# The memory's values made before the second mixer, and the router and the experts' tokens taken from x itself

## The chip, the cores and the metric

The kernel runs on one core of a Trainium2 chip. The metric is the device time of one execution in microseconds (us), taken as the median of several runs. The core has a matrix engine (TensorE, PE in the profile), a vector engine (DVE), a scalar engine (ACT), GpSimd (POOL), and SyncE (SP), which here issues nearly all the transfers from DRAM.

## What is computed

Two transformer blocks follow one another on 256 tokens of width 1024, all in float32. The first has two layers: an mLSTM mixer with a dense FFN, and then an HGRN2 mixer with eight experts, of which each token takes two. The second block is attention with three branches, one of which reads a memory of 256 rows, and a dense FFN. What the change touches is this part (`ada` is a linear map of a conditioning vector that gives six vectors for each layer):

```
hn = rmsnorm(x, norm1_w) * (1 + scale1) + shift1
x  = x + gate1 * hgrn2_mixer(hn)                 # ends with "@ h_w_out", the out-projection
hn = rmsnorm(x, norm2_w) * (1 + scale2) + shift2
logits = hn @ router_w                           # 1024 x 8
top_logits, top_idx = top_k(logits, 2);  top_w = softmax(top_logits)
x  = x + gate2 * sum_e gates[:, e] * swiglu(hn, wg[e], wu[e], wd[e])
...
mkv = rms_norm(mem, g_mem) @ w_mem_kv            # 1024 x 1024: keys 0..511, values 512..1023
mk, mv = split(mkv);  mk = rms_norm(heads(mk), g_k_mem)
```

## The kernel before

The activations are kept transposed, as `x` of 128 partitions by 8 chunks by 256 tokens. Every float32 operand of a large product is split into a high and a low part (`whi`/`wlo` for weights, `act_hi`/`act_lo` for activations); ACT writes the high part as a rounded copy and DVE the low part as a difference. `mm3` then issues three passes, high by high, low by high, high by low. Small products are issued by `mm` on plain float32 operands; each such instruction stands as two matmuls in the trace. In an order listing it is still one, so `x4` there is `x8` in the trace.

Weights come as tiles of up to 1 MB in the order that `all_weights` (line 186 on) yields them. `load` puts each in one of four `raw` buffers (some in one of two `raw2` buffers), `parts_of` splits it into one of three `whi` and three `wlo` buffers, and `prepare` keeps a depth of one or two tiles split ahead of the products. Between the FFN's products one tile of `ada_w` after another is also loaded, into `raw2`, and summed by DVE (`ada_step`).

A scheduler puts each engine's instructions in an order that it decides when the program is built; each engine then works through its list strictly in that order, and waits at an instruction until its inputs and its buffer are there. `hold` and `behind` keep a step back until a named instruction has been issued: after a normalization (`normed`) the next tiles' splits wait for its last instruction.

A normalization sums squares over all 1024 values of a token: ACT squares each chunk, POOL adds the first of them up, PE sums over partitions with a column of ones (`token_sums`), DVE works out the inverse root in about ten small steps (`rsqrt`, names `st1v`, `st1y`), PE spreads it over the partitions (`spread`: a broadcast column times the identity), and DVE and ACT write the normalized chunks.

Around the change the program runs thus. After the first FFN comes `normed` and then `hgrn`, the second mixer. In the out-projection that ends the mixer, `memory_norm` loads the memory `memT`, sums its squares and writes its split `yeh`/`yel`. Then `normed` writes the experts' input, `moe` makes the logits with the split router weights (24 products), turns the input from chunks to token order with 32 products with `identr`, takes the two largest logits of each token (`first_max`, a chain of small DVE steps), and counts tokens for each expert (five products on `mask`). `memory` issues 48 products for the keys K, `head_norm` normalizes these, and 48 more products make the values V. A branch (line 1159) then asks whether an expert has over 128 tokens; every engine passes it. Behind it `experts` gathers the tokens for each pair of experts with 32 products on `disp`.

Of the kernel before, what the change touches and what calls it, by code (L numbers as in the profile page):

```python
# [20 lines left out]
P = 128  # L21
# [117 lines left out]
class Kernel:  # L139
# [61 lines left out]
    def all_weights(self):  # L201
# [19 lines left out]
        yield from ffn(a["ffn_w_gate"], a["ffn_w_up"], a["ffn_w_down"], FF)  # L221
        yield from columns("h_w_in", 1024, 1536, 0, 512, 2048, 2560, 3072, 3584)
        yield from columns("h_w_out", 0, 512)
        yield from columns("w_mem_kv_2", 0, 512)
# [331 lines left out]
    def out_proj(self, act, gate, between=None):  # L556
        self.stat_begin()
        self.depth = 2
        for g in range(2):
            self.proj_t(act, between=between, ends=lambda banks, cb: self.resid(banks[cb // 2][:, cb % 2, :], 4 * g + cb, gate))  # L560
# [142 lines left out]
    def run(self):  # L703
# [4 lines left out]
        with tc.tile_pool(name="cond", bufs=1) as pool:  # L708
# [19 lines left out]
            self.ffn(act, self.mod_part(0, 5), lambda f: self.ada_step(f * 30 / 33))  # L728
            self.tap("x2", x)
            self.ada_owed = 0.0  # L730
            self.hold = [[self.last_resid]] * 2
            self.ada_until(32)
            with tc.tile_pool(name="hgrn", bufs=1) as hgrn:
                act = self.normed(x, self.stat_end(), self.gain(1, 1, self.vec("n1", 8, 8)), self.mod_part(1, 0))
                act = self.hgrn(hgrn, act)
            self.ada_until(48)
        self.wide = False
        with tc.tile_pool(name="moe", bufs=1) as pool:
            kv = self.ctx.enter_context(tc.tile_pool(name="memkv", bufs=1, side="right"))
            self.mk = self.t(kv, [P, 4, S], "mk")  # L740
            self.mv = self.t(kv, [P, 2, 512], "mv")
            mem = self.memory_norm(pool)
            self.out_proj(act, self.mod_part(1, 2))
            self.tap("x3", x)
            act = self.normed(x, self.stat_end(), self.gain(1, 4, self.vec("n2", 8, 8)), self.mod_part(1, 3))
            self.moe(pool, act, mem)
# [19 lines left out]
    def memory_norm(self, pool):  # L766

        m = self.raw(self.a["memT"].rearrange("p (c s) -> p c s", c=DC))
        self.stat_begin()
# [319 lines left out]
    def moe(self, pool, act, mem):  # L1089
        nc, a, tc = self.nc, self.a, self.tc  # L1090
        lgp = self.bank()
        lgt = self.t(pool, [8, S], "lgt")
        lg = self.t(pool, [P, 2, 8], "lg")
        self.small(lgp[:8, :S], self.router_w, act)
        nc.vector.tensor_copy(lgt, lgp[:8, :S])
        for tt in range(2):
            nc.tensor.transpose(lgp[:, S + tt * 8 : S + tt * 8 + 8], lgt[:, tt * P : (tt + 1) * P], self.cst("ident")[:8, :8])
        nc.vector.tensor_copy(lg.rearrange("p a b -> p (a b)"), lgp[:, S : S + 16])

        xt = [self.t(pool, [P, 2, D], n, 1, F32R) for n in ("xth", "xtl")]  # L1100
        for tt in range(2):
            for half in range(2):
                for i in range(2):
                    ps = self.bank()
                    for c in range(4):
                        self.mm(ps[:, c * P : (c + 1) * P], act[i][:, half * 4 + c, tt * P : (tt + 1) * P], self.identr, c == 0)
                    dst = xt[i][:, tt, half * 512 : (half + 1) * 512]
                    if i == 0:
                        self.act(dst, ps, AF.Copy)
                    else:  # L1110
                        nc.vector.tensor_copy(dst, ps)
# [17 lines left out]
        e2, w1, w2 = (sm(n, (P, 2)) for n in ("e2", "w1", "w2"))  # L1129
# [352 lines left out]
```

## Time and profile before

| | |
|---|---|
| runs, median (lowest to highest) | 1469.27 us (1464.16 to 1472.32), 3 runs |
| the profiled execution's own time | 1472.68 us |
| its span in the trace | 1470.9 us |
| mean granted clock of PE, share of full | 0.969 |
| PE busy | 1416.9 us, 96% of the span |
| DVE, ACT, POOL busy | 1122.9, 837.9, 33.8 us |
| transfers | 343.49 MB, mean 234 GB/s |

Busy time of PE counts matmuls that overlap in the pipeline, so the work of a product is read from the distance between the starts of two neighbours. The numbers of the stretch in which the change lies are in three parts of the span: the middle and the end of the first FFN (about 265 to 379 us), the second out-projection (524 to 548 us), and the routing up to the experts' first product (548 to 598 us).

### The profile page before, as it was taken

The numbers are of one execution on the slowest core, as the hardware profiler recorded it, in microseconds if no ns is written. First come the engines' busy times: TensorE is split into PE (matmuls) and PEld (weight loads), VectorE is DVE, ScalarE is ACT, GpSimd is POOL, SyncE is SP. The second block draws the span as 40 slices with busy tenths as digits, with TensorE's granted clock in tenths as the row PEclk, the third lists the DMA queues.
The fourth block names the chain that finished last, engine by engine and source line by source line (L and its number), as shares of the span: only waits on it lengthen the run. The fifth ranks groups of instructions, "written<-read, shape, count | busy, mean of one in ns | idle before, by whom it ended". The sixth has DMA issues, their size and how long they took to land.

```text
span 1470.9 us, 23270 instructions
## 1 busy us (share of the span) xinstructions
PE 1416.9 (96%) x9356; PEld 1293.3 (88%) x9356; DVE 1122.9 (76%) x1741; ACT 837.9 (57%) x1197; POOL 33.8 (2%) x38
## 2 busy tenths in 40 slices
PE   5999899999899998999999999999999999999998
PEld 4789899999899986888888888888878899999998
DVE  6875798888687867698798897888776777765554
ACT  2652454344695555777787777777555455544332
POOL 1000100000000020000000000000000000100000
PEclk7987899999899999899999999999999999999999
DMA  8975579998454144599799898996425344555542
GB/s 336 342 270 185 176 278 355 348 348 328 153 174 142 59 156 131 193 362 361 271 363 330 306 350 324 329 352 227 154 86 188 128 146 142 172 175 198 173 144 87
DMA packets 149507, 343.49 MB, mean 234 GB/s; under 512 B 5904, under 2 KB 27280, under 8 KB 149136
## 3 DMA queue, kind: packets, MB, share of 16 engines
q1 hardware_dynamic: 148240, 341.00, 65.9%
q8 instruction: 75, 1.23, 0.3%
q10 hardware_dynamic: 1152, 0.94, 0.2%
q14 instruction: 40, 0.33, 0.1%
HBM read 340.86 MB, written 1.05 MB: 232 GB/s over the span
## 4 chain that ended last, share of the span: by engine, by line
PE 57%; ACT 1%; DVE 1%; issue 0%; ACTq 0%
PE acc L165 38%; PE ps L165 17%; PE ps L1222 1%; ACT whi L175 0%; PE ps L1313 0%; DVE wlo L181 0%; PE ps L700 0%; ACT e L175 0%; ACT L175 0%; PE ps L1438 0%; DVE yel L178 0%; ACT yeh L175 0%; ACT sg L175 0%; DVE ss L679 0%; DVE nm L1306 0%
## 5 line engine op out<-in xcount | busy, mean ns | idle before, releaser
L181 DVE TENSOR_TENSOR wlo<-raw,whi 128x1024 fp32r<-128x1024 f32 (+2 forms) x564 | 647.2, 1184 | 147.7 <-ACT whi L175 147.0
L175 ACT ACTIVATE whi<-raw 128x1024 fp32r<-128x1024 f32 (+2 forms) x564 | 547.8, 1016 | 321.6 <-PE acc L165 183.5
L165 PE MATMUL acc<-act_hi,whi 128*128 128x256 f32 x1344 | 385.1, 288 | 2.7 <-ACT act_hi L175 2.4
L165 PE MATMUL acc<-act_lo,whi 128*128 128x256 f32 x1344 | 385.0, 287 | 0.0
L165 PE MATMUL acc<-act_hi,wlo 128*128 128x256 f32 x1344 | 383.1, 285 | 1.3 <-DVE wlo L181 1.3
L165 PEld LDWEIGHTS acc<-act_hi,whi 128*128 128x128 f32 x1344 | 258.6, 193 | 4.7 <-ACT act_hi L175 3.0
L165 PEld LDWEIGHTS acc<-act_hi,wlo 128*128 128x128 f32 x1344 | 258.9, 193 | 1.6 <-DVE wlo L181 1.5
L165 PEld LDWEIGHTS acc<-act_lo,whi 128*128 128x128 f32 x1344 | 259.0, 193 | 1.1 <-issue 0.4
L165 PE MATMUL acc<-whi,act_hi 128*128 128x512 f32 (+1 forms) x560 | 216.1, 386 | 1.8 <-DVE conv L178 1.7
L165 PE MATMUL acc<-wlo,act_hi 128*128 128x512 f32 (+1 forms) x560 | 215.2, 384 | 0.0
L165 PE MATMUL acc<-whi,act_lo 128*128 128x512 f32 (+1 forms) x560 | 214.5, 383 | 0.0
L165 PEld LDWEIGHTS acc<-whi,act_hi 128*128 128x128 f32 x560 | 105.2, 188 | 21.4 <-issue 2.2
L165 PEld LDWEIGHTS acc<-wlo,act_hi 128*128 128x128 f32 x560 | 105.2, 188 | 19.3 <-DVE wlo L181 0.6
L165 PEld LDWEIGHTS acc<-whi,act_lo 128*128 128x128 f32 x560 | 105.1, 188 | 18.8
L485 DVE SCALAR_TENSOR_TENSOR raw<-raw,cond 128x1024 f32<-128x1024 f32 x96 | 115.3, 1230 | 6.4 <-DMA raw<-in_ada_w_dram 6.4
L165 PE MATMUL ps<-hh,whi 128*128 128x256 f32 x352 | 99.6, 283 | 1.5 <-DVE x L178 1.5
L165 PE MATMUL ps<-hl,whi 128*128 128x256 f32 x352 | 99.5, 283 | 0.0
L165 PE MATMUL ps<-hh,wlo 128*128 128x256 f32 x352 | 99.4, 283 | 0.0
L165 PE MATMUL ps<-wlo,hth 128*128 128x512 f32 x176 | 69.0, 392 | 0.0
L165 PEld LDWEIGHTS ps<-hh,whi 128*128 128x128 f32 x352 | 67.4, 192 | 1.7 <-DVE x L178 1.7
L165 PE MATMUL ps<-whi,htl 128*128 128x512 f32 x176 | 68.8, 391 | 0.0
L165 PE MATMUL ps<-whi,hth 128*128 128x512 f32 x176 | 67.5, 393 | 0.0
(355 smaller groups left out, 1777.5 us busy)
## 6 DMA issues: line engine op xcount, KB each, us to landing
raw<-in_ada_w_dram SPq DMA_DIRECT2D x48, 1024.0 KB, 6.3
raw<-in_moe_w_down_dram SPq DMA_DIRECT2D x40, 1024.0 KB, 5.7
raw<-in_moe_w_up_dram SPq DMA_DIRECT2D x32, 1024.0 KB, 7.3
raw<-in_moe_w_gate_dram SPq DMA_DIRECT2D x32, 1024.0 KB, 7.6
raw<-in_w_in_dram SPq DMA_DIRECT2D x26, 1024.0 KB, 5.1
raw<-in_h_w_in_dram SPq DMA_DIRECT2D x16, 1024.0 KB, 5.7
raw<-in_m_w_in_dram SPq DMA_DIRECT2D x12, 1024.0 KB, 7.4
raw<-in_moe_w_gate_dram SPq DMA_DIRECT2D x16, 768.0 KB, 5.5
```

The costliest lines, as they stand in the source:

```text
L165: self.nc.tensor.matmul(out, l, r, start=start, stop=True, skip_group_check=True)
L175: return self.nc.scalar.activation(out, in_, f, **k)
L181: return self.nc.vector.tensor_tensor(out, a, b, op=op)
L485: last = self.nc.vector.scalar_tensor_tensor(w[:, i, :], in0=w[:, i, :], scalar=1.0, in1=self.cond, op0=ALU.mult, op1=ALU.mult, accum_out= ...
L1222: nc.tensor.transpose(hps[:, f * P : (f + 1) * P], h[:, f * P : (f + 1) * P], self.cst("ident"))
```

## The change

The values V are made right behind the first FFN. The memory is loaded and normalized in the middle of that FFN (at its 61st quarter step), the two tiles of `w_mem_kv` with V's columns come before the mixer's weights, and V goes to a DRAM tile, from which it is read back later. The memory is loaded and normalized a second time in the out-projection, for K. `memory_norm` now makes the scaled memory by a plain ACT copy, then a rounded ACT copy and a POOL subtraction, where it was one rounded ACT copy and one DVE step.

The experts' input is no longer normalized in chunks. `route_begin` multiplies the router weights by the gain (`gw`) and writes the gain as a diagonal matrix for each chunk (`gdiag`), both on POOL; spreads the shift over a row (`srow`, eight plain float32 products); and works out the shift's part of the logits (`sw`, eight more). `route_add` adds each chunk of x to the logits as soon as the out-projection has ended it, 16 plain float32 products in all. `moe` then turns x to token order with 16 plain float32 products on `gdiag`; the inverse root comes in per token, by DVE, as it reads the result.

In `experts` the 32 gathering products of a pair on `disp` now stand ahead of the small products of the gates (`gps`) and of the way back (`bps`), where they stood behind them.

```diff
@@ -219,9 +219,10 @@
...
+        yield from columns("w_mem_kv_2", 512)
         yield from columns("h_w_in", 1024, 1536, 0, 512, 2048, 2560, 3072, 3584)
         yield from columns("h_w_out", 0, 512)
-        yield from columns("w_mem_kv_2", 0, 512)
+        yield from columns("w_mem_kv_2", 0)
...
@@ -553,11 +554,23 @@
-    def out_proj(self, act, gate, between=None):
+    def out_proj(self, act, gate, between=None, also=None):
...
+            def products():
+                if also:
+                    also(c)
+                sums()
...
@@ -722,16 +735,30 @@
...
-            self.router_w = self.load_small(self.cp, "router_w")
+            self.router_w = self.load_small(self.cp, "router_w", True)[0]
...
+            self.mv_kept = dram.tile([P, 2, 512], F32, tag="mv", name="mv_kept", bufs=1)
+            with tc.tile_pool(name="mem", bufs=1) as pool:
+                mem = []
+
+                def between(f):
+                    self.ada_step(f * 30 / 33)
+                    mem.append(self.memory_norm(pool, "acc") if len(mem) == 60 else None)
+
+                self.ffn(act, self.mod_part(0, 5), between)
+                m, by = mem[60]
...
+                act = self.normed(x, self.stat_end(), self.gain(1, 1, self.vec("n1", 8, 8)), self.mod_part(1, 0))
+                mv = self.t(pool, [P, 2, 512], "mv")
+                for tt, bank in enumerate(self.proj_tok(m)):
+                    self.act(mv[:, tt, :], bank, AF.Copy, scale=by[:, tt, :])
+                nc.scalar.dma_start(self.mv_kept, mv)
             with tc.tile_pool(name="hgrn", bufs=1) as hgrn:
-                act = self.normed(x, self.stat_end(), self.gain(1, 1, self.vec("n1", 8, 8)), self.mod_part(1, 0))
                 act = self.hgrn(hgrn, act)
...
@@ -739,11 +766,12 @@
...
+            nc.scalar.dma_start(self.mv, self.mv_kept)
+            self.route_begin(pool)
             mem = self.memory_norm(pool)
-            self.out_proj(act, self.mod_part(1, 2))
+            self.out_proj(act, self.mod_part(1, 2), also=self.route_add)
             self.tap("x3", x)
-            act = self.normed(x, self.stat_end(), self.gain(1, 4, self.vec("n2", 8, 8)), self.mod_part(1, 3))
-            self.moe(pool, act, mem)
+            self.moe(pool, mem)
...
@@ -763,19 +791,23 @@
...
-        return self.scaled(m, self.vec("g_mem"), tiles), self.stat_tokens()
+        g = self.vec("g_mem")
+        for c in range(DC):
+            t = self.t(self.tp, [P, S], "sq", 4)
+            self.act(t, m[:, c, :], AF.Copy, scale=g[:, c : c + 1])
+            self.act(tiles[0][:, c, :], t, AF.Copy)
+            self.nc.gpsimd.tensor_tensor(tiles[1][:, c, :], t, tiles[0][:, c, :].bitcast(F32), op=ALU.subtract)
+        return tiles, self.stat_tokens()
...
     def memory(self, pool, act, by):
         self.head_norm(pool, self.proj_tok(act), 4, self.mk, self.vec("gk_mem"), by=by)
-        for tt, bank in enumerate(self.proj_tok(act)):
-            self.act(self.mv[:, tt, :], bank, AF.Copy, scale=by[:, tt, :])
...
@@ -1086,29 +1118,49 @@
...
+    def route_begin(self, pool):
...
+        nc.gpsimd.tensor_tensor(self.gw, self.router_w, g.unsqueeze(2).to_broadcast([P, DC, 8]), op=ALU.mult)
+        for c in range(DC):
+            nc.gpsimd.tensor_tensor(self.gdiag[:, c, :], self.cst("ident"), g[:, c : c + 1].to_broadcast([P, P]), op=ALU.mult)
+        for half in range(2):
+            ps = self.bank()
+            for i in range(4):
+                self.spread(ps[:, i * P : (i + 1) * P], shift[:, 4 * half + i : 4 * half + i + 1], i == 0)
+            self.act(self.srow[:, half * 512 : half * 512 + 512], ps, AF.Copy)
+        ps = self.bank()
+        self.lgp = ps[:, :16].rearrange("p (a e) -> p a e", a=2)
+        for c in range(DC):
+            self.mm(ps[:, 16:24], shift[:, c : c + 1].to_broadcast([P, P]), self.router_w[:, c, :], c == 0)
+        self.sw = self.t(self.cp, [P, 8], "sw")
+        self.act(self.sw, ps[:, 16:24], AF.Copy)
+
+    def route_add(self, c):
+        for tt in range(2):
+            self.mm(self.lgp[:, tt, :], self.x[:, c, tt * P : (tt + 1) * P], self.gw[:, c, :], False)
...
+                    self.mm(ps[:, c * P : (c + 1) * P], self.x[:, cc, tt * P : (tt + 1) * P], self.gdiag[:, cc, :], c == 0)
+                xps.append(ps)
+        r = self.stat_tokens()
         for tt in range(2):
...
+            self.stt(lg[:, tt, :], self.lgp[:, tt, :], r[:, tt, :], self.sw, ALU.mult, ALU.add)
...
-                for i in range(2):
-                    ps = self.bank()
-                    for c in range(4):
-                        self.mm(ps[:, c * P : (c + 1) * P], act[i][:, half * 4 + c, tt * P : (tt + 1) * P], self.identr, c == 0)
...
+        for n, ps in enumerate(xps):
+            half, tt = n // 2, n % 2
+            sl = slice(half * 512, half * 512 + 512)
+            t = self.t(self.tp, [P, 512], "h", 2)
+            self.stt(t, ps, r[:, tt, :], self.srow[:, sl], ALU.mult, ALU.add)
+            self.split(xt[0][:, tt, sl], xt[1][:, tt, sl], t)
...
+        self.wide = True
+        self.hold = [[routed]]
+        self.memory(pool, *mem)
         self.depth = 1
-        self.wide = True
-        self.memory(pool, *mem)
...
```

PE from the first FFN to the second mixer. Before: the FFN's last products (`ps`), the token sums, the spread, and the mixer's first products.

```order
L165 MATMUL ps_1943<-hh_3361,wlo_3370 128x256
L165 MATMUL acc_3479<-cst_base_69,sq_3524 128x1 x2
L165 MATMUL acc_3479<-cst_base_69,sq_3534 128x1 x2
L165 MATMUL acc_3479<-cst_base_69,sq_3545 128x1 x2
L165 MATMUL acc_3479<-cst_base_69,sq_3556 128x1 x2
L165 MATMUL acc_3479<-cst_base_69,sq_3567 128x1 x2
L165 MATMUL ps_3591<-cst_base_69,st1y_3579 128x128 x2
L165 MATMUL acc_3644<-act_hi_3596,whi_3425 128x256
```

After: the memory's normalized copy (`yeh`, `yel`) times V's weights stands between the sums.

```order
L165 MATMUL ps_1945<-hh_3441,wlo_3450 128x256
L165 MATMUL acc_3559<-cst_base_69,sq_3604 128x1 x2
L165 MATMUL acc_3708<-whi_3505,yeh_2443 128x512
L165 MATMUL acc_3559<-cst_base_69,sq_3614 128x1 x2
L165 MATMUL acc_3708<-wlo_3506,yeh_2443 128x512
L165 MATMUL acc_3708<-whi_3505,yel_2444 128x512
L165 MATMUL acc_3559<-cst_base_69,sq_3625 128x1 x2
L165 MATMUL acc_3709<-whi_3505,yeh_2443 128x512
L165 MATMUL acc_3709<-wlo_3506,yeh_2443 128x512
```

Further V products and the spread of the inverse root follow, eight products behind the last sum (a part):

```order
L165 MATMUL acc_3708<-wlo_3506,yeh_2443 128x512
L165 MATMUL acc_3708<-whi_3505,yel_2444 128x512
L165 MATMUL ps_3668<-cst_base_69,st1y_3656 128x128 x2
L165 MATMUL acc_3709<-whi_3505,yeh_2443 128x512
L165 MATMUL acc_3709<-wlo_3506,yeh_2443 128x512
```

The last V products and the mixer's first (`act_hi` is the normalized input):

```order
L165 MATMUL acc_3709<-wlo_3582,yeh_2443 128x512
L165 MATMUL acc_3709<-whi_3581,yel_2444 128x512
L165 MATMUL acc_3795<-act_hi_3673,whi_3712 128x256
L165 MATMUL acc_3795<-act_lo_3674,whi_3712 128x256
L165 MATMUL acc_3796<-act_hi_3673,whi_3712 128x256
```

The 48 V products stand between the FFN's last product and the mixer's first, 15 of them ahead of the spread and 33 behind it.

PE at the start of the second out-projection. `r4y` is the inverse root of the mixer's heads. Before, the rows on `sq` are the memory's sums:

```order
L165 MATMUL acc_5160<-act_lo_4459,whi_5034 128x256
L165 MATMUL ps_4821<-cst_base_69,r4y_4809 128x128 x4
L165 MATMUL ps_4827<-cst_base_69,r4y_4809 128x128 x4
L165 MATMUL ps_4969<-cst_base_69,sq_4984 128x1 x2
L165 MATMUL ps_4969<-cst_base_69,sq_4989 128x1 x2
L165 MATMUL ps_4969<-cst_base_69,sq_4993 128x1 x2
L165 MATMUL acc_5160<-act_hi_4458,wlo_5035 128x256
```

After, `mod` is the shift:

```order
L165 MATMUL acc_5235<-act_hi_4609,whi_4988 128x256
L165 MATMUL ps_4972<-cst_base_69,r4y_4960 128x128 x4
L165 MATMUL ps_4978<-cst_base_69,r4y_4960 128x128 x4
L165 MATMUL ps_5132<-cst_base_69,mod_77 128x128 x4
L165 MATMUL ps_5138<-cst_base_69,mod_77 128x128 x4
L165 MATMUL ps_5144<-router_w_1398,mod_77 128x8 x8
L165 MATMUL ps_5157<-cst_base_69,sq_5172 128x1 x2
L165 MATMUL ps_5157<-cst_base_69,sq_5177 128x1 x2
L165 MATMUL ps_5157<-cst_base_69,sq_5181 128x1 x2
L165 MATMUL acc_5235<-act_lo_4610,whi_4988 128x256
L165 MATMUL acc_5235<-act_hi_4609,wlo_4989 128x256
```

Eight spreads of the shift (two rows of four) and eight products of the shift with the router weights have come in between the spreads of `r4y` and the memory's sums.

PE at the branch. Before: V's last products, the branch, the gates' products, and then the gathering on `xth`/`xtl`.

```order
L165 MATMUL acc_5569<-wlo_5573,yeh_4997 128x512
L165 MATMUL acc_5569<-whi_5572,yel_4998 128x512
L1157 TENSOR_LOAD mosti_5469
L1159 COMPARE_AND_BRANCH
L165 MATMUL ps_5658<-gate_5454,disp_5657 128x1
L165 MATMUL ps_5670<-identr_75,disp_5657 128x128
L165 MATMUL ps_5658<-gate_5454,disp_5657 128x1
L165 MATMUL ps_5670<-identr_75,disp_5657 128x128
```

After: K's last products, the transposes of the normalized keys `h`, the branch, and the gathering.

```order
L165 MATMUL acc_5614<-whi_5463,yeh_5185 128x512
L165 MATMUL acc_5614<-wlo_5464,yeh_5185 128x512
L165 MATMUL acc_5614<-whi_5463,yel_5186 128x512
L713 MATMUL ps_5703<-cst_base_69,h_5701 128x128 x4
L713 MATMUL ps_5711<-cst_base_69,h_5709 128x128 x4
L1218 TENSOR_LOAD mosti_5583
L1220 COMPARE_AND_BRANCH
L165 MATMUL ps_5745<-disp_5738,xth_5550 128x256 x2
L165 MATMUL ps_5745<-disp_5738,xtl_5551 128x256 x2
```

V's 48 products are gone from here, and with them the work among which the transposes of the keys stood before: these now stand alone between K's last product and the branch.

## Rows read from the trace of the kernel before

**Rows 1.** The page: busy times, the chain that ended last, and the costliest DVE group

```profile
PE 1416.9 (96%) x9356; PEld 1293.3 (88%) x9356; DVE 1122.9 (76%) x1741; ACT 837.9 (57%) x1197; POOL 33.8 (2%) x38
...
PE 57%; ACT 1%; DVE 1%; issue 0%; ACTq 0%
...
L181 DVE TENSOR_TENSOR wlo<-raw,whi 128x1024 fp32r<-128x1024 f32 (+2 forms) x564 | 647.2, 1184 | 147.7 <-ACT whi L175 147.0
```

**Rows 2.** ACT in the first FFN, in time: start, duration, work, [idle before <-releaser]

```profile
266.54 2.01 ACT L175 ACTIVATE whi<-raw 128x1024 fp32r<-128x1024 f32 x2 [2.74 <-PE ps L165]
...
272.30 2.01 ACT L175 ACTIVATE whi<-raw 128x1024 fp32r<-128x1024 f32 x2 [3.75 <-PE ps L165]
```

**Rows 3.** Busy time by stretch in the FFN (length; PE, PEld, DVE, ACT, POOL; clock; DMA)

```profile
265.00:275.00 10.00, 10.00 (x87) 10.00 (x86) 6.97 (x10) 4.02 (x4) 0.00 (x0) 1.00 1.03 402
```

**Rows 4.** POOL in time: runs of five additions of squares

```profile
8.58 6.63 POOL L410 TENSOR_TENSOR sq<-sq,sq 128x256 f32<-128x256 f32 x5 [7.25 <-ACT sq L175]
...
520.99 4.02 POOL L410 TENSOR_TENSOR sq<-sq,sq 128x256 f32<-128x256 f32 x5 [148.28 <-ACT sq L175]
```

**Rows 5.** PE in time, from the FFN to the second mixer

```profile
370.37 0.28 PE L165 MATMUL ps<-hh,wlo 128*128 128x256 f32 x1
...
370.99 3.46 PE L165 MATMUL acc<-cst_base,sq 128*128 128x1 f32 x20 [0.34 <-POOL sq L410]
...
376.48 1.22 PE L165 MATMUL ps<-cst_base,st1y 128*128 128x128 f32 x4 [2.03 <-DVE st1y L178]
...
378.89 0.79 PE L165 MATMUL acc<-act_hi,whi 128*128 128x256 f32 x2 [1.19 <-ACT act_hi L175]
```

**Rows 6.** Busy time by stretch at other places, columns as in rows 3

```profile
102.00:105.00 3.00, 3.00 (x16) 2.82 (x16) 3.00 (x7) 0.75 (x2) 0.00 (x0) 0.57 0.11 38
...
372.00:385.00 13.00, 9.78 (x55) 9.26 (x54) 8.16 (x27) 4.71 (x11) 0.72 (x1) 0.61 0.63 236
...
526.00:533.00 7.00, 7.00 (x37) 7.00 (x36) 5.10 (x16) 2.87 (x6) 0.00 (x0) 0.53 0.00 0
...
585.00:589.00 4.00, 0.15 (x1) 0.15 (x1) 2.25 (x5) 1.39 (x3) 0.00 (x0) 0.77 0.53 192
...
589.00:598.00 9.00, 9.00 (x45) 9.00 (x46) 2.32 (x6) 7.07 (x17) 0.00 (x0) 0.54 0.33 120
```

**Rows 7.** PE in time, start of the second out-projection

```profile
524.56 2.73 PE L165 MATMUL ps<-cst_base,r4y 128*128 128x128 f32 x16 [1.98 <-DVE r4y L178]
...
527.08 2.56 PE L165 MATMUL ps<-cst_base,sq 128*128 128x1 f32 x12
```

**Rows 8.** PE in time, plain float32 products elsewhere

```profile
96.64 0.82 PE L165 MATMUL ps<-p,v 128*128 128x256 f32 x4
...
509.29 1.05 PE L165 MATMUL ps<-qt,kfull 128*128 128x128 f32 x8
```

**Rows 9.** PE in time, from the out-projection to the experts

```profile
549.01 0.61 PE L165 MATMUL ps<-cst_base,sq 128*128 128x1 f32 x4 [0.70 <-POOL sq L410]
...
570.69 0.58 PE L165 MATMUL ps<-mask,cst_moe 128*128 128x8 f32 x4 [0.91 <-ACT sg L175]
...
583.96 0.39 PE L165 MATMUL acc<-wlo,yeh 128*128 128x512 f32 x1
...
584.19 0.39 PE L165 MATMUL acc<-whi,yel 128*128 128x512 f32 x1
...
588.85 0.58 PE L165 MATMUL ps<-gate,disp 128*128 128x1 f32 x2 [4.28 <-ACTq L1159]
...
597.94 0.40 PE L165 MATMUL acc<-whi,act_hi 128*128 128x512 f32 x1
```

**Rows 10.** ACT in time, the memory's keys and values

```profile
572.79 0.69 ACT L175 ACTIVATE sg<-acc,st1y 128x512 f32<-128x512 f32 x1 [2.15 <-PE acc L165]
...
580.29 1.36 ACT L175 ACTIVATE mk<-ps,vecs 128x512 f32<-128x512 f32 x2
...
583.93 1.37 ACT L175 ACTIVATE mv<-acc,st1y 128x512 f32<-128x512 f32 x2 [2.29 <-PE acc L165]
```

More of the change, by code (lines that the diff above doesn't have):

```diff
@@ L554, in resid, with chunk @@
         return self.square(chunk)
-    def out_proj(self, act, gate, between=None):
+    def out_proj(self, act, gate, between=None, also=None):
         self.stat_begin()
         self.depth = 2
+        def chunk(ps, c):
+            sums = self.resid(ps, c, gate)
+            def products():
+                if also:
+                    also(c)
+                sums()
+            return products
         for g in range(2):
-            self.proj_t(act, between=between, ends=lambda banks, cb: self.resid(banks[cb // 2][:, cb % 2, :], 4 * g + cb, gate))
+            self.proj_t(act, between=between, ends=lambda banks, cb: chunk(banks[cb // 2][:, cb % 2, :], 4 * g + cb))
     def ffn(self, act, gate=None, between=None, factor=None):
@@ L1090, in moe @@
+    def route_add(self, c):
+        for tt in range(2):
+            self.mm(self.lgp[:, tt, :], self.x[:, c, tt * P : (tt + 1) * P], self.gw[:, c, :], False)
+    def moe(self, pool, mem):
         nc, a, tc = self.nc, self.a, self.tc
-        lgp = self.bank()
-        lgt = self.t(pool, [8, S], "lgt")
         lg = self.t(pool, [P, 2, 8], "lg")
-        self.small(lgp[:8, :S], self.router_w, act)
-        nc.vector.tensor_copy(lgt, lgp[:8, :S])
+        xps = []
+        for half in range(2):
+            for tt in range(2):
+                ps = self.bank("acc" if half else "ps")
+                for c in range(4):
+                    cc = half * 4 + c
+                    self.mm(ps[:, c * P : (c + 1) * P], self.x[:, cc, tt * P : (tt + 1) * P], self.gdiag[:, cc, :], c == 0)
+                xps.append(ps)
+        r = self.stat_tokens()
@@ L1128, in moe @@
         first_max(l2, m2, oh2)
-        e2, w1, w2 = (sm(n, (P, 2)) for n in ("e2", "w1", "w2"))
-        self.tt(e2, m2, m1, ALU.subtract)
-        self.act(e2, e2, AF.Exp)
-        self.ts(w1, e2, 1.0, ALU.add)
-        nc.vector.reciprocal(w1, w1)
-        self.tt(w2, w1, e2, ALU.mult)
         mask, gate, pos, tmp = (sm(n) for n in ("mask", "gate", "pos", "tmp"))
-        self.tt(mask, oh1, oh2, ALU.add)
-        self.tt(gate, oh1, bcast(w1), ALU.mult)
-        self.tt(tmp, oh2, bcast(w2), ALU.mult)
-        self.tt(gate, gate, tmp, ALU.add)
+        routed = self.tt(mask, oh1, oh2, ALU.add).ins
         pps = self.bank()
@@ L1150, in moe @@
         nc.vector.tensor_copy(mosti, most)
+        for n, ps in enumerate(xps):
[4 more added lines that the diff above has]
+            self.split(xt[0][:, tt, sl], xt[1][:, tt, sl], t)
+        e2, w1, w2 = (sm(n, (P, 2)) for n in ("e2", "w1", "w2"))
+        self.tt(e2, m2, m1, ALU.subtract)
+        self.act(e2, e2, AF.Exp)
+        self.ts(w1, e2, 1.0, ALU.add)
+        nc.vector.reciprocal(w1, w1)
+        self.tt(w2, w1, e2, ALU.mult)
+        self.tt(gate, oh1, bcast(w1), ALU.mult)
+        self.tt(tmp, oh2, bcast(w2), ALU.mult)
+        self.tt(gate, gate, tmp, ALU.add)
+        self.wide = True
+        self.hold = [[routed]]
+        self.memory(pool, *mem)
         self.depth = 1
-        self.wide = True
-        self.memory(pool, *mem)
         while len(self.loaded) < 2:
@@ L1186, in experts @@
             disp = self.t(pool, [P, 2, 2, P], "disp", 2, F32R)
+            for i in range(2):
+                e = 2 * pr + i
+                for tt in range(2):
+                    self.ts(disp[:, tt, i, :], self.cst("iota"), pos[:, tt, e : e + 1], ALU.is_equal, mask[:, tt, e : e + 1], ALU.mult)
+            xe = self.act_tiles()
+            for c in range(DC):
+                ps = self.bank()
+                for n in range(2):
+                    for tt in range(2):
+                        self.mm(ps[:, n * S : (n + 1) * S], xt[n][:, tt, c * P : (c + 1) * P], disp[:, tt, :, :].rearrange("p e s -> p (e s)"), n + tt == 0)
+                self.act(xe[0][:, c, :], ps[:, :S], AF.Copy)
+                self.act(xe[1][:, c, :], ps[:, S:], AF.Copy)
             gps = self.bank()
```

41 lines of the change are left out of this document (14 added, 27 removed).

## The prediction

> **What bounds the kernel now.** I read the page first: which engine is busy and whose work the chain that ended last consists of [rows 1]. The reader is to see that PE is busy for 96% of the span and that 57% of it is PE work on that chain, while DVE and ACT stand at 76% and 57%. So what counts is what is added to PE's list, where PE waits, and at which clock it runs. Then I read the busy time by stretch, for the clock [rows 3, 6], and PE in order of time at the three places of the change [rows 5, 7, 9], where the number behind "[" is the idle time before a row. PE is full in the middle of the FFN, whose clock is 1.00 [rows 3]; it is idle for 0.34, 2.03 and 1.19 us around the token sums and the spread ahead of the second mixer [rows 5], for 1.98 us ahead of the spreads in the out-projection [rows 7], and for 4.28 us at the branch [rows 9]. Behind such places the granted clock falls: 0.61, 0.53 and 0.54 of full [rows 6], the lower of the levels being 1.2 GHz and the upper 2.4.
>
> Two prices are used throughout. A pass with 512 columns takes 0.23 us at the upper clock, from the start at 583.96 to the next [rows 9], so 48 of them, V or K, take 11.0. A plain float32 product of 128 columns is two records; the four at 509.29 took 1.05 with the tail of the last [rows 8], so I take 0.24 for one at the upper clock. At the lower clock eight spreads took 2.52 us from their start to the next row, 0.315 each, and six token sums 2.56 with a tail, 0.40 each [rows 7].
>
> **The change part by part.** The sum is made against the profiled execution, 1472.68 us with a span of 1470.9; it lies 3.4 above the median of 1469.27, and I put the difference on the median.
>
> 1. *The memory in the FFN.* ACT ended a weight tile at 268.55 and waited for PE until 272.30, when PE gave a buffer free, having ended a tile [rows 2]. The squares go into that gap, POOL's five additions behind them, and PE's order has the six token sums right behind that tile's last product. Five additions took 4.0 us in one place and 6.6 in another, waits for their inputs within [rows 4]. With two squares first (half of the 0.69 us that a square of 512 columns took [rows 10] and something for the wait, 0.8 in all), the last one ends at 273.4 to 276.0, so that PE, which reaches it at 272.3, waits 1.1 to 3.7 us and then works 6 x 0.24 = 1.4. I take the 4.0, which is the row nearer in time and kind (a stretch within the dense products): **+2.5**; without a wait 1.4, at the other end 5.1. Behind these, ACT has 16 copies before the next weight tile. They fit into its free 6 us of 10 [rows 3], and PE has two split tiles ahead of it. If that cover is gone, PE waits for ACT's whole pair of copies, 2.0 us [rows 2].
>
> 2. *V ahead of the second mixer.* PE's last FFN product ended at 370.65 [rows 5]. Behind it now come ten token sums (2.4 at the upper clock), 48 passes (11.0) and two spreads (0.5): PE can't reach the mixer before 384.6. The sums are not held up, since V's passes lie among them, and 33 passes cover the normalization. The mixer's first weight tile is held behind the normalization, because V's tiles took the buffers in which it lay split before; half a tile takes ACT 1.0 us [rows 2], and I add 0.9 for it: 385.5, against 378.89 [rows 5]. But PE no longer rests there. A mean clock of 0.61 over 13 us means some 10 us at the lower level, that is to about 382 [rows 6], so 3.2 us of the mixer's products ran at half speed, and that loss of 1.6 goes. 385.5 - 378.89 - 1.6 = **+5.0**; +4.1 if the split is in time, +7 if it comes two half tiles late. V's eviction and its transfer to DRAM (0.5 MB) lie on ACT and its queue beside the mixer; the small constants of the mixer are queued behind that transfer, and are needed only after its first projections.
>
> 3. *The out-projection.* Behind the spreads of `r4y`, PE now has eight spreads of the shift and eight products with the router weights before the sums: 8 x 0.315 + 8 x 0.40 = 5.7, at the lower clock that stands there [rows 6]. Nothing covers them: PE had no idle time between these rows and the products behind. Ten of the 16 logit products fall among the out-projection's own, 10 x 0.24 = 2.4. **+8.1**; at the upper clock the sixteen take 3.8 and the sum is 6.2. POOL's diagonals and subtractions are not waited for, as K comes much later, and DVE's eight steps fewer are not on the path.
>
> 4. *From the out-projection's last product to the experts' first.* Before, 549.01 - 0.70 = 548.31 to 597.94: 49.6 us [rows 9]. After: six logit products, six sums and 16 diagonal products, 28 x 0.24 = 6.7; K, 11.0, with the five count products on `mask`, 1.2, in it. The two largest logits are found meanwhile; PE has 31 passes of K (7 us) ahead of the count, so I charge no wait. Now comes what was hidden. The normalization of the keys ran from the second square at 572.79 to the end of `mk` at 580.29 + 1.36 = 581.65, 8.9 us [rows 10], while PE made V. Now PE has nothing but eight transposes there, and the branch stands behind them: 8.9 in full. Then the branch, 4.28 from V's last product less 0.7 for the half of the eviction `mv` behind it [rows 9, 10]: 3.5. Then the gathering at the lower clock, 588.85 to 597.94, 9.1 [rows 6, 9]. Together 6.7 + 12.2 + 8.9 + 3.5 + 9.1 = 40.4, that is **-9.2**. It is more (-14) if the chain loses the two weight differences that lie in it (2 x 1.18 of the 8.9 [rows 1]) and the gathering is waited for without the small products, now behind it (13 of 45 records, 2.6 [rows 6]); less (-6) if the transposes at the lower clock and the engines' passing of the branch in a row add 3.
>
> 5. *The clock in K.* In the trace a run of plain float32 products from 96.64 on, without idle time, was followed by a clock of 0.57 from 102 on [rows 6, 8]. The 6.7 us of part 4 are such a run. If the clock falls as at 526 to 533, seven us at 0.53 lose 3.3; if not, nothing. The nearest row speaks for a fall, but there more such products followed. I take half: **+1.7**.
>
> A second transfer of the memory (1 MB) and V's way back come at stretches whose transfers are at 0.00 to 0.6 of the engines' time [rows 6]: nothing. In the experts the reordered small products are as many as before: nothing.
>
> Sum: 2.5 + 5.0 + 8.1 - 9.2 + 1.7 = +8.1; 1469.27 + 8.1 = 1477.4 us.
>
> The Trainium skill, "SBUF — State Buffer", section "Who interferes with whom", says that a VectorE instruction with two inputs in SBUF and a GpSimd instruction that reads SBUF exclude each other for the whole instruction. The spread between 4.0 and 6.6 us of rows 4 agrees with it, without proving it. It speaks against putting 13 POOL steps into the FFN, and stands behind the first rival.
>
> **The rivals.**
> *POOL against DVE in the FFN.* Each of the 13 POOL steps (0.8 us, a fifth of 4.0 [rows 4]) holds up a weight difference: 10.4 us of DVE where it has about 9 free (3 of 10 in some 30 us [rows 3]), 1.4 too many, which PE waits. The sums come at the late end (5.1 for 2.5), and K, too, is at the lower clock (3.3 for 1.7). 8.1 + 2.6 + 1.4 + 1.6 = 13.7, with the late split of part 2 (2.0) 15.7: 1485. For it: DVE is the second busiest. Against: PE has two split tiles in hand.
> *The clock does not fall.* If PE, now without V's gap and with more to do at the out-projection, is granted 1.00 there, the sixteen products take 3.8 for 5.7, the 7 us at 0.53 give back 3.3, and part 5 is nothing: 8.1 - 1.9 - 3.3 - 1.7 = +1.2, 1470.5, not slower. It decides from a clock of 0.9 at the spreads on. For it: from 533 on PE has the upper clock. Against: the idle time of 1.98 ahead of the spreads stays, and after the run of rows 8 the clock did fall.
> *The chain is short.* ACT and DVE have little else then, so that the normalization of the keys takes the low end of part 4, -14.2; with the clock held as above the sum is -3.8, with V's split in time and no wait in the FFN -5.8, and with the gathering at the upper clock, 6.5 us halved, -9: 1460. Against: the chain's own steps are as many as before, and each waits for the one ahead.
>
> **How the numbers follow.** Within 0.5%, 7.3 us, a measurement of this kernel can't be told from no change. My forecast (3 to 12 us slower, 1472 to 1481) has a chance of 0.47, the first rival 0.20, the second 0.17, the third 0.16. The forecast lies about the mark of 7.3: 0.21 of it is same and 0.26 slower. Of the second 0.15 is same and 0.02 faster, of the third 0.03 and 0.13. Faster 0.15, same 0.39, slower 0.46. The low ends (1.4 + 4.1 + 6.2 - 14.3) give -2.6, the high ones 5.1 + 7.0 + 8.1 - 6 + 3.3 = 17.5; the range reaches below the first, for part of the third rival: 1462 to 1487.
>
> **What would show it.** In the profile after: PE idle 1 to 4 us for a POOL `sq` in the FFN; the mixer's first product some 15 us behind the FFN's last one, and at the upper clock; about 10 us from the `r4y` spreads to the products behind the sums; 40 us from the out-projection's last product to the experts' first, with one gap of some 12 us around the transposes of the keys and the branch. The prediction is wrong if that last stretch takes under 34 us or over 46, if the clock at the spreads is 1.00, or if the FFN's products lose more than 6 us.

## The result, and the profile after

The changed kernel takes 1485.35 us (median of 5 runs, 1480.96 to 1487.13), the kernel before beside it 1467.94 (1464.16 to 1472.32): a ratio of 1.0125 with a 95% interval of 1.0101 to 1.015. It is slower, as forecast, but by 17.4 us where 8.1 stood.

Its page reads much like before's [rows 1]: PE has as large a share of the span and of the chain. PE is busy 8.2 us longer, with 46 instructions more. How much of that is work and how much the clock, and where it lies, the averages don't show.

```profile
PE 1425.1 (96%) x9402; PEld 1303.6 (88%) x9402; DVE 1122.1 (76%) x1730; ACT 845.4 (57%) x1221; POOL 54.1 (4%) x68
...
PE 57%; ACT 1%; DVE 1%; issue 0%; ACTq 0%
```

So I cut the span at marks that PE leaves in both traces, and compared the stages. The FFN goes from its first product to the first on its last down tile, the boundary from there to the mixer's first product, the mixer to the spread of `r4y`, the out-projection to its last product, the routing to the experts' first. In us, before and then the differences from it:

| | ahead | FFN | boundary | mixer | out-proj. | routing | experts on | span |
|---|---|---|---|---|---|---|---|---|
| before | 178.0 | 191.7 | 9.2 | 145.7 | 23.6 | 49.8 | 873.0 | 1470.9 |
| after | +0.4 | +7.7 | +10.7 | +3.5 | +4.7 | -11.5 | -1.1 | +14.4 |
| route_only | -1.2 | +1.4 | -1.0 | +0.1 | +6.4 | -8.0 | +2.2 | -0.2 |
| v_only | +0.3 | +5.0 | +10.7 | +5.2 | -0.8 | -4.6 | -1.8 | +14.1 |
| late_sums | +0.3 | +3.5 | +10.7 | +2.2 | +3.8 | -11.6 | +1.9 | +10.9 |
| route_early | -7.3 | +0.1 | -1.1 | +1.1 | +2.4 | -6.9 | +0.4 | -11.4 |
| sums_first | -0.9 | +2.1 | +7.5 | -0.8 | +4.6 | -11.6 | -1.3 | -0.4 |
| best | -5.9 | +0.9 | -0.3 | +0.9 | +3.5 | -7.8 | -1.2 | -9.9 |

The labels are the experiments below. Where a stage holds the same work in two kernels, it repeats to 1.4 us in FFN, boundary and mixer of before, route_only and route_early, but only to 2.7 in the FFN of after and v_only. The part ahead of the FFN, which no kernel touches, moves by up to 7 us from one execution to the next, with a mean granted clock of 0.86 to 0.95 over its first 170 us, so one span says less than its stages. Before's own profiled execution lies 4.7 above its median of these runs, and after's 1.8 above its own, which is why 14.4 in the traces are 17.4 in the runs.

The mark between mixer and out-projection does not cut all kernels at the same product. Eleven of the out-projection's own products, 0.12 us each, stand ahead of the spreads of `r4y` in before and behind them in after, v_only and late_sums. Cut at the same products, after loses 4.8 in the mixer and 3.4 in the out-projection.

PE in time in the changed kernel, against [rows 5, 7, 9] (start, duration, work, [idle before]):

```profile
275.33 1.05 PE L165 MATMUL acc<-cst_base,sq 128*128 128x1 f32 x8 [1.88 <-POOL sq L411]
...
360.43 0.39 PE L165 MATMUL ps<-hh,wlo 128*128 128x256 f32 x1 [1.04 <-DVE wlo L181]
...
379.13 0.93 PE L165 MATMUL acc<-cst_base,sq 128*128 128x1 f32 x4 [0.39 <-POOL sq L411]
379.92 0.77 PE L165 MATMUL acc<-whi,yeh 128*128 128x512 f32 x1
380.49 0.85 PE L165 MATMUL acc<-cst_base,sq 128*128 128x1 f32 x4
...
389.71 0.61 PE L165 MATMUL ps<-cst_base,st1y 128*128 128x128 f32 x4
...
397.68 0.30 PE L165 MATMUL acc<-act_hi,whi 128*128 128x256 f32 x1
...
433.75 0.39 PE L165 MATMUL acc<-act_hi,whi 128*128 128x256 f32 x1 [0.94 <-ACT whi L175]
...
534.03 0.62 PE L165 MATMUL acc<-act_hi,whi 128*128 128x256 f32 x3 [1.55 <-ACT act_hi L175]
...
546.87 2.05 PE L165 MATMUL ps<-cst_base,r4y 128*128 128x128 f32 x16 [1.85 <-DVE r4y L178]
548.76 1.95 PE L165 MATMUL ps<-cst_base,mod 128*128 128x128 f32 x16
550.55 1.85 PE L165 MATMUL ps<-router_w,mod 128*128 128x8 f32 x16
552.25 1.72 PE L165 MATMUL ps<-cst_base,sq 128*128 128x1 f32 x12
...
575.14 0.51 PE L165 MATMUL ps<-gw,x 128*128 128x8 f32 x4
...
581.30 0.48 PE L165 MATMUL acc<-whi,yeh 128*128 128x512 f32 x1
...
600.36 1.97 PE L713 MATMUL ps<-cst_base,h 128*128 128x128 f32 x8 [6.61 <-DVE h L181]
606.35 1.19 PE L165 MATMUL ps<-disp,xth 128*128 128x256 f32 x4 [4.02 <-DVE disp L187]
...
613.46 0.47 PE L165 MATMUL acc<-whi,act_hi 128*128 128x512 f32 x1
```

And its busy time by stretch, columns as in [rows 3]; the third number from the end is the granted clock:

```profile
275.00:278.00 3.00, 2.67 (x19) 2.67 (x19) 0.76 (x3) 2.54 (x7) 1.41 (x3) 0.81 0.30 116
278.00:290.00 12.00, 12.00 (x94) 12.00 (x94) 11.72 (x18) 7.95 (x16) 4.53 (x7) 0.91 0.69 254
...
380.00:390.00 10.00, 10.00 (x35) 8.61 (x35) 1.62 (x10) 0.42 (x1) 0.00 (x0) 0.53 0.72 286
390.00:400.00 10.00, 9.47 (x49) 7.85 (x49) 8.92 (x19) 6.95 (x12) 0.00 (x0) 1.00 0.01 2
...
536.00:540.00 4.00, 4.00 (x23) 4.00 (x23) 1.19 (x1) 1.82 (x5) 0.00 (x0) 0.57 0.40 98
...
545.00:553.00 8.00, 6.15 (x56) 6.13 (x55) 4.93 (x10) 2.68 (x7) 2.21 (x3) 1.00 0.01 3
553.00:557.00 4.00, 4.00 (x23) 4.00 (x22) 2.26 (x12) 3.50 (x7) 0.91 (x3) 0.57 0.01 1
...
575.00:581.30 6.30, 6.30 (x59) 6.30 (x58) 2.62 (x13) 2.62 (x4) 0.00 (x0) 1.00 0.54 180
...
582.00:594.00 12.00, 11.75 (x57) 9.35 (x55) 11.64 (x34) 6.92 (x10) 0.00 (x0) 1.00 0.12 29
```

Four stretches of dense products run at the lower level: some 3.4 us behind the FFN's wait (from 276.9 to 280.3), some 10 us between the FFN and the mixer, some 3.4 in the mixer behind the wait at 534.03, and some 3.4 in the out-projection. (Most of the gathering of the experts' tokens does too, as before.) Between 380 and 390 PE is busy all the time and starts 35 instructions; in the 9.47 busy microseconds behind, 49.

### The profile page after: what moved, and what is told of

Read it like the earlier page. It is cut to its first block, busy times and chain, and to the rows that moved or that the text cites. A ratio compares the mean times of both kernels' runs of the same rounds, so it can differ in the third digit from the quotient of the medians.

```text
span 1485.3 us, 23430 instructions
## 1 busy us (share of the span) xinstructions
PE 1425.1 (96%) x9402; PEld 1303.6 (88%) x9402; DVE 1122.1 (76%) x1730; ACT 845.4 (57%) x1221; POOL 54.1 (4%) x68
## 4 chain that ended last, share of the span: by engine, by line
PE 57%; ACT 1%; DVE 1%; issue 0%; ACTq 0%
PE acc L165 39%; PE ps L165 17%; PE ps L1286 1%; PE ps L1377 0%; ACT whi L175 0%; PE ps L713 0%; ACT L175 0%; DVE wlo L181 0%; ACT e L175 0%; PE ps L1502 0%; DVE yel L178 0%; ACT yeh L175 0%; DVE nm L1370 0%; ACT lfe L175 0%; ACT sq L175 0%
## 5 line engine op out<-in xcount | busy, mean ns | idle before, releaser
L165 PEld LDWEIGHTS ps<-hh,wlo 128*128 128x128 f32 x352 | 67.1, 192 | 1.2 <-DVE wlo L181 1.2
```

What stands on the lines that cost most here:

```text
L165: self.nc.tensor.matmul(out, l, r, start=start, stop=True, skip_group_check=True)
```

## Experiments

My theory after the result: V at its new place costs PE the whole of its passes, because the clock is low there, and at its old place it was nearly free; the routing's own change gains, and gives that back at the out-projection. The main rival: each part costs about what the prediction said, and something else in the FFN or the routing made the difference.

### route_only: the routing's part alone, V where it was before

```diff
 (all_weights, memory and the call of the mixer as before)
+            self.route_begin(pool)
             mem = self.memory_norm(pool)
-            self.out_proj(act, self.mod_part(1, 2))
+            self.out_proj(act, self.mod_part(1, 2), also=self.route_add)
```

> The second part of the change alone: tokens, router and logits from x as after, but V made at the branch as before and nothing of the memory in the FFN. My theory, from the two traces: V's move is what costs (some 20 us up to the out-projection), and routing from x pays. The out-projection then costs 4.7 us more than before, the stretch from its last product to the experts takes 6.2 + 12.1 + 11.0 + 3.5 + 8.5 = 41.3 us for 49.6, and the pairs of experts give 1.1: about -4.7 us against before, ratio 0.997. The rival, that the new float32 products are what costs and taking V from the branch is what pays, expects over 1.003.

Measured: 1465.52 us, ratio 0.9985 (0.9956 to 1.0013), no change that can be told. The theory's 0.997 lies in the interval, the rival's 1.003 does not. The stages say why nothing is gained: -8.0 in the routing, +6.4 in the out-projection, where the theory took over the 4.7 of the changed kernel.

```profile
523.79 3.04 PE L165 MATMUL ps<-cst_base,r4y 128*128 128x128 f32 x16 [1.95 <-DVE r4y L178]
526.62 2.60 PE L165 MATMUL ps<-cst_base,mod 128*128 128x128 f32 x16
...
588.78 0.39 PE L165 MATMUL ps<-disp,xth 128*128 128x256 f32 x1 [4.46 <-ACTq L1206]
```

Here the clock was low twice in the out-projection (columns as above):

```profile
523.00:528.00 5.00, 4.21 (x23) 4.24 (x24) 3.02 (x6) 3.50 (x6) 1.16 (x2) 0.66 0.00 0
528.00:531.00 3.00, 3.00 (x30) 3.00 (x29) 0.95 (x2) 0.68 (x2) 0.00 (x0) 1.00 0.00 0
531.00:539.00 8.00, 8.00 (x44) 8.00 (x44) 4.63 (x14) 5.08 (x14) 5.18 (x12) 0.57 0.01 4
```

What follows: with V behind K the routing took 49.8 - 8.0 = 41.8 us, and without it, in the changed kernel, 38.3. V's 48 passes, 11.0 us of PE work, cost 3.5 there: the rest lay over the keys' normalization. (The next run gives 4.6 for the same price in the old routing.)

### v_only: V's part alone, the routing as before

```diff
 (out_proj, moe and the experts as before)
+                self.ffn(act, self.mod_part(0, 5), between)
+                m, by = mem[60]
...
+                for tt, bank in enumerate(self.proj_tok(m)):
+                    self.act(mv[:, tt, :], bank, AF.Copy, scale=by[:, tt, :])
```

> The first part alone: the memory normalized in the FFN and V made behind it, the routing as before. My theory: 7 us lost in the FFN, 9 at the boundary to the second mixer, up to 5 in the mixer; at the branch 11 of V go and most of the 8.9 of the keys' chain comes to light: +17 to +19 us, ratio 1.012. The rival (taking V from the branch pays, the float32 products cost): under +8 us, ratio below 1.006.

Measured: 1485.2 us, 1.0113 (1.0075 to 1.0152). This is the theory's time, and far from the rival's. V's move makes the whole loss: +5.0, +10.7 and +5.2 in the FFN, the boundary and the mixer against -4.6 in the routing. Of the 11.0 us that left the routing, 6.4 came back as waits that V had covered; the first is the wait for the normalized keys, as long as in the changed kernel:

```profile
599.86 1.94 PE L701 MATMUL ps<-cst_base,h 128*128 128x128 f32 x8 [6.60 <-DVE h L181]
...
605.52 0.56 PE L165 MATMUL ps<-gate,disp 128*128 128x1 f32 x2 [3.73 <-DVE disp L187]
```

### late_sums: the changed kernel, the memory's token sums in the FFN six quarter steps later

```diff
-                    mem.append(self.memory_norm(pool, "acc") if len(mem) == 60 else None)
+                    n = len(mem)
+                    if n == 60:
+                        self.late = self.memory_norm(pool, "acc", True)
+                    mem.append(None)
+                    if n == 66:
+                        for sums in self.late[1]:
+                            sums()
+                        mem[60] = self.late[0], self.stat_tokens()
```

> The kernel after, with the memory's token sums in the FFN issued 36 passes later (4.2 us) on PE, so that POOL's additions are done by then; the sums stay. Theory A, an idle PE is what lets the clock fall: the 1.88 us of idle go and with them the lower clock from 276.9 on (about 3.3 us at half): -3 to -4 us against after, about 1481.5. Theory B, the plain float32 sums let it fall: -1.9. Theory C, the FFN's loss is in later waits on split tiles: 0.

Measured: 1482.78 us, 1.0097 (1.0065 to 1.0129), whose interval overlaps the changed kernel's; the trace tells them apart. PE no longer waits for the sums:

```profile
276.96 1.39 PE L165 MATMUL acc<-cst_base,sq 128*128 128x1 f32 x12
```

and the clock stays up, where the changed kernel had 0.81 and 0.91:

```profile
275.00:278.00 3.00, 3.00 (x29) 3.00 (x28) 1.23 (x1) 2.97 (x6) 0.74 (x1) 1.00 0.92 365
278.00:290.00 12.00, 12.00 (x103) 12.00 (x103) 11.69 (x19) 9.53 (x20) 6.45 (x7) 1.00 0.55 197
```

The FFN's loss falls from 7.7 to 3.5. The same 60 dense products around the sums show it without the scatter of the rest: they take 7.0 to 7.1 us in the four kernels without the memory in the FFN; with the sums among them it is 12.1 and 12.2 with the wait (after, from 273.17 to 285.29, and v_only), and 8.5 with the late sums (late_sums, from 272.57 to 281.02, and sums_first). So the sums cost 1.4 and the wait 3.7: 1.9 of idle time, and half of some 3.4 us at the lower level. Theory A's time came. The six sums without the wait (twelve records) did not bring the clock down. The boundary stayed at +10.7.

Theory C is not empty either. The wait at 360.43 above stands in all four kernels that make V behind the FFN and in none of the others, and costs each 1.3 us from one product to the same one. There DVE's low part waits for ACT's high part, and ACT had waited for the transfer of the tile:

```profile
355.94 2.01 ACT L175 ACTIVATE whi<-raw 128x1024 fp32r<-128x1024 f32 x2 [2.56 <-DMA raw<-in_ffn_w_down_dram]
```

What made that transfer late, no run separates.

### route_early: route_only, with the shift's router products right behind the mixer's last token sum

```diff
+            if g == 1:
+                with self.behind(self.last_mm):
+                    early()          # the eight products of the shift with the router weights
             for b in range(2):
                 pb =
```

> Routing from x alone, with the eight products of the shift with the router weights put on PE right behind the mixer's last token sum, where PE is idle for 1.85 us ahead of the spreads of r4y. If that idle time and the lower clock that follows it belong together: -1.7 and -1.4, 3 us below routing alone; if the clock falls for another reason: -1.7; if nothing is hidden: 0.

Measured: 1465.75 us, 0.9991 (0.9967 to 1.0015). The idle time ahead of `r4y` is gone and the out-projection's loss is down from 6.4 to 2.4; 1.0 of this went with the eight products into the mixer, so that 3.0 remain, the first case's time. The lower level lasts some 3.4 us where it lasted some 10 in routing alone. But the clock fell all the same:

```profile
513.45 1.93 PE L165 MATMUL ps<-router_w,mod 128*128 128x8 f32 x16
...
517.32 3.21 PE L165 MATMUL ps<-cst_base,r4y 128*128 128x128 f32 x16
```

```profile
511.00:516.00 5.00, 5.00 (x44) 4.80 (x43) 1.68 (x10) 1.64 (x6) 0.02 (x1) 1.00 0.63 210
516.00:520.00 4.00, 4.00 (x23) 4.00 (x22) 0.66 (x1) 2.21 (x7) 3.63 (x5) 0.57 0.00 0
```

So idle time is not needed: here PE was busy for all of 511 to 520, a good part of it with plain float32 products of few columns. An account by idle time alone does not hold. Nor does one by such products alone: in the changed kernel the 6.2 us from 575.14 on are nothing but plain float32 products, and the clock stayed at 1.00 (575.00:581.30 above).

### sums_first: late_sums, with V's passes held behind the last of the ten token sums at the boundary

```diff
                 m, by = mem[60]
+                last_sum = self.last_product
...
-                for tt, bank in enumerate(self.proj_tok(m)):
+                for tt, bank in enumerate([x for x in self.proj_tok_halves(m, [last_sum])][-1]):
```

(`proj_tok_halves` is `proj_tok` with `behind(last_sum)` around its products.)

> The kernel with the late token sums, and V's 48 passes held behind the last of the ten token sums at the end of the FFN, where after they lie among them. After, the clock is at its lower level for 10.2 us there, and V's first passes run in it. Theory D, plain float32 sums strewn among the passes keep the clock low: it is low for 3.4 to 6.8 us only, and the stretch from the FFN's last product to the mixer takes 17 to 19 us for 19.9. Theory E, the fall belongs to the wait of 1.5 us for x ahead of the sums, whatever follows: low for 10 us again, and 19.9 or more.

Measured: 1474.45 us, 1.0052 (1.0019 to 1.0086). The boundary is 16.7 us for 19.9. The same sums and passes, in another order:

```profile
372.19 2.39 PE L165 MATMUL acc<-cst_base,sq 128*128 128x1 f32 x20 [0.41 <-POOL sq L430]
...
374.45 0.57 PE L165 MATMUL acc<-whi,yeh 128*128 128x512 f32 x1
...
387.50 0.28 PE L165 MATMUL acc<-act_hi,whi 128*128 128x256 f32 x1
```

```profile
374.00:379.00 5.00, 5.00 (x21) 4.13 (x21) 1.96 (x11) 0.00 (x0) 0.00 (x0) 0.66 1.03 414
379.00:390.00 11.00, 11.00 (x60) 9.49 (x59) 10.35 (x20) 8.71 (x15) 0.00 (x0) 1.00 0.18 49
```

The clock is low for about 3.4 us (from 374.7 to 378.1) instead of 10. Half of the 6.8 us that this saves is 3.4; 3.2 were measured. That is theory D's account. Theory E's wait is there unchanged (1.47 us), so E does not hold for the 10 us. This is one trace; the three with the sums strewn (after, v_only, late_sums) all have some 10 us. With the sums in a block and no V, before has some 10 too and route_only some 7, but there PE rested behind the sums. The second gain was not looked for: the mixer takes 0.8 less than before instead of 2.2 to 5.2 more. In the changed kernel PE waits there for ACT (433.75 and 534.03 above), and at neither place in sums_first. ACT in time at the second place, the changed kernel:

```profile
532.40 1.06 ACT L175 ACTIVATE whi<-raw 128x1024 fp32r<-128x1024 f32 x1 [1.95 <-PE acc L165]
533.37 1.14 ACT L175 ACTIVATE act_hi<-yo 128x512 fp32r<-128x512 f32 x2
```

and in sums_first:

```profile
517.37 0.63 ACT L175 ACTIVATE act_hi<-yo 128x512 fp32r<-128x512 f32 x1 [0.81 <-PE acc L165]
518.26 0.60 ACT L175 ACTIVATE cross<-ps 128x512 f32<-128x512 f32 x1 [0.26 <-PE ps L165]
518.75 1.05 ACT L175 ACTIVATE whi<-raw 128x1024 fp32r<-128x1024 f32 x1
```

In the first, the split `whi` stands ahead of `act_hi` and waits 1.95 us for PE to give its buffer free, while PE waits for that `act_hi`. In sums_first, and before, `act_hi` comes first. Three kernels with V strewn among the sums have the first order, and sums_first the second; the scheduler chose both. The rows show order and wait together; I did not swap the order by itself, so that the one makes the other is argued.

At the first place the rows show something else, which the prediction named and put at nothing. V's transfer to DRAM and the load of the mixer's constants are issued by ACT one behind the other, and ACT stands still until the first has landed:

```profile
407.43 1.06 ACT L175 ACTIVATE whi<-raw 128x1024 fp32r<-128x1024 f32 x1 [2.12 <-DMA mv_kept<-mv]
```

From there to the split that PE awaits at 433.75 ACT rests for only 0.54 us. It stands still for 2.1 to 2.3 us in the three kernels that have PE's wait, 1.3 in sums_first, and not at all in before. That this delay makes PE's wait is not tested.

### best: an attempt to keep the routing's gain alone

```diff
 (route_early, and the row of the shift spread in PE's idle time behind the FFN and kept in DRAM)
+            self.srow_kept = dram.tile([P, D], F32, tag="srow", name="srow_kept", bufs=1)
...
+        nc.scalar.dma_start(self.srow, self.srow_kept)
```

> Routing from x alone, V at the branch, with both groups of shift products in places where PE is idle in the kernel before: the eight for the router behind the mixer's last token sum, the eight spreads of the shift row between the token sums and the spread of the inverse root behind the FFN (2.0 us idle), the row kept in DRAM meanwhile. If these idle times hide them, the stretch around the out-projection goes from +6.4 (routing alone) to about +1, the boundary stays at 8 to 9 us: 4 to 5 us below before, ratio 0.997. If the longer run of plain float32 products at the boundary lowers the clock for longer, that is lost again: 1.000.

Measured: 1468.72 us, 0.9999 (0.9965 to 1.0033), with before at 1465.39 on that chip (the ratio is not that of the two medians, which is 1.002). It is the time of the second case, but not by its reason: the boundary stayed at 8.9 us. The routing keeps -7.8 and the out-projection is still at +3.5: PE now waits 2.24 us in its middle for a residual sum on DVE, and the clock falls again.

```profile
542.25 0.39 PE L165 MATMUL acc<-act_hi,whi 128*128 128x256 f32 x1 [2.24 <-DVE x L178]
```

No version that I ran beats the kernel before by more than can be measured.

## Why the prediction was right in sign and too small

**The memory in the FFN, +2.5, measured +7.7.** The wait of 1 to 4 us for POOL's `sq` is there, 1.88. The failed step is "a wait, and then 6 x 0.24": the price of the wait left out what it does to the clock, some 1.7 us in the products behind. Without the wait, clock and idle time, 3.5 remain (late_sums) and 2.1 (sums_first): 1.4 for the sums, 1.3 for the split that came late at 360.43, of which the prediction had nothing, and the scatter of that stage.

**V ahead of the mixer, +5.0.** Booked by stages, the prediction was +6.6 for the boundary and -1.6 for the mixer; they came at +10.7 and +3.5. The failed step is "2.4 at the upper clock" and 48 passes at 0.23. The passes ahead of the spread stood 0.43 apart instead (387.32 to 387.75, 388.17), as the clock was at 0.53. I had used the low clock of the old boundary [rows 6] only as a loss that would go, on the ground that PE no longer rests; but the sums that stood under it came along, strewn over seven microseconds (379.13 to 386.32). The late split cost 0.53 (398.85) for the 0.9 assumed. In the mixer the 1.6 did come back (its first products run at 1.00); against it stand some 3 us of new waits on ACT and DVE, and a stretch of low clock behind the last of them. The waits at 534 go with ACT's other order, of which the prediction had nothing, as it looked at the order only where the code changes. The one at 433.75 comes behind ACT's 2.12 us of standing still for V's transfer, which the prediction named and put at nothing.

**The out-projection, +8.1, measured +4.7.** The mis-sized term is the clock: the sixteen products came at 1.00, 3.5 us (548.76 to 552.25) for 5.7. That is the second rival's condition, a clock of 0.9 or more at the spreads, and its price for this place. But the clock fell afterwards, at 553, for some 3.4 us where it had been low for some 7 [rows 6], and half of what this saves is 1.7. The 2.2 and the 1.7, with 0.7 for three passes of K that now stand behind the stage's end, make up about the 4.7 between the forecast and the 3.4 at the same products. The idle time of 1.85 stayed.

**The routing, -9.2, measured -11.5.** The structure held: small products 6.2 us (575.14 to 581.30) for 6.7, K 12.4 for 12.2, then the wait for the keys, 6.61, and the one at the branch, 4.02 (its row names DVE's `disp`, the first step behind the branch), which with the transposes make the gap of some 12 us. The gathering took 7.1 (606.35 to 613.46) for 9.1, near the low end named for it (6.5), without the small products ahead and with the clock back up for the last 2 us.

**The clock in K, +1.7, measured 0.** 582 to 594 ran at 1.00. So did the run of plain products ahead of it, though it is unbroken from 575.14 to 581.30, nearly as long as the prediction had it (6.7). The row taken for it [rows 8] was no measure: what stood at half was the step from a run of plain products to a fall of the clock, and here none followed.

**The rivals.** The first rival's 1485 is the time that came, for another reason: POOL's subtractions do hold DVE up, but no PE wait in that stretch follows from it; the one at 360.43 comes 78 us behind POOL's last step there. The small steps of the inverse root, 0.16 alone, take 0.65 to 0.69 beside them. DVE in time in the changed kernel, then POOL:

```profile
278.33 0.69 DVE L178 SCALAR_TENSOR_TENSOR st1h<-st1h,st1v 128x2 f32<-128x2 f32 x1
...
282.58 0.16 DVE L178 SCALAR_TENSOR_TENSOR st1y<-st1h,st1y 128x2 f32<-128x2 f32 x1
```

```profile
276.86 5.67 POOL L806 TENSOR_TENSOR yel<-sq,yeh 128x256 fp32r<-128x256 f32 x8 [1.59 <-ACT yeh L175]
```

The last step, behind POOL's end at 282.53, is short again. By the Trainium skill, "SBUF — State Buffer", section "Who interferes with whom", a VectorE instruction with two SBUF inputs and a GpSimd instruction that reads SBUF exclude each other; the steps of about 0.7 beside subtractions of 5.67 / 8 = 0.71 agree. The effect is there and did not decide.

**The signs that it named.** Of the three by which it was to be wrong, two came: the clock at the spreads was 1.00, and the FFN lost 7.7, over 6. The third did not: the last stretch took 38.3. The mixer's first product came 18.9 us behind the FFN's last one, for 15, and the stretch from the `r4y` spreads to the products behind the sums took 7.0, for 10.

So the sign rested on what was sized well (V's passes no longer hidden, the chain of the keys bare), and the size was missed by 5.2 in the FFN and 9.2 in boundary and mixer, less 3.4, 2.3 and 1.7 elsewhere: 7.0 in all. With the -0.7 of the two untouched ends this is the 14.4 - 8.1 = 6.3 between trace and forecast. That the misses of 14.4 and 7.4 have opposite signs, and so left the total this near, is luck.

## What to carry to other kernels

Before work is moved to "where PE rests", ask what it covered at its old place: V cost 3.5 to 4.6 us over the keys' chain and the branch, and 7.5 to 10.7 at the boundary where it went. Look at what the dense products behind a wait of PE, or among small plain products, lose at the lower clock, and not at its own length alone; in these traces such products cost less in one block than strewn among dense ones. And read every engine's order in the stage behind the change too, since a scheduler may reorder what the code leaves alone.

## What was unexpected of the hardware

A granted clock at the lower level did not need idle time: in route_early it fell in 516 to 520, PE busy throughout, behind a run of plain float32 products. Such a run did not always bring it: 6.2 us of them in the changed kernel left it at 1.00. Nor did being busy end it: between 380 and 390 PE never rested and had 0.53, with dense passes of 512 columns and sums of one column in turn up to 386.3 and passes alone behind; with the same work in two blocks it was back up after some 3.4 us. And six such sums without a wait, in the FFN of late_sums, left it at 1.00. The Trainium skill, "TensorE: Matmul & The Clock Gate", Part 1, says that "the default state is throttled, and activity releases the throttle": the stretch of 10 us at 0.53, 100% busy in the profile, does not go with this if the profile's busy time is taken for the activity. What in the strewn order goes with the longer stretch, no run here separates.
